# A gated recurrence block: decays scanned backward in place of their reciprocals, and the pooling's products made among the heads

## The chip, the cores and the metric

The kernel runs on one core of one Trainium2 chip. The metric is the device time of one execution in microseconds (us); three executions were timed before the change. One more execution was recorded by the hardware profiler: its page, and answers from its trace, are what this document quotes. PE is TensorE (matmuls), PEld its weight loads, DVE VectorE, ACT ScalarE, POOL GpSimd, and SP the queue that issues nearly all DMAs.

## The reference

One decoder layer on 1024 tokens of width 1024, all float32:

```python
proj = x @ w_in            # -> q, f, i, og, pool_v, gate_a, gate_b, each 1024 wide
# recurrence, 8 heads of 128, in chunks of 16 tokens:
qf = silu(q) * 128**-0.5;  f = lb + (1 - lb) * sigmoid(f);  k = 1 - f;  G = cumsum(log f) within a chunk
scores = tril((qf * exp(G)) @ (k * exp(-G)).T);   o_intra = scores @ v
state = exp(G_last) * state + (k * exp(G_last - G)).T @ v;   o_inter = (qf * exp(G)) @ state
o = rmsnorm_per_head(o_intra + o_inter) * g * sigmoid(og);   a = o @ w_a
# pooling, 4 groups of 256 channels, windows 2, 4, 8, 16:
pooled = causal_mean_w(pool_v) - pool_v;   b = (pooled @ w_pool[group]) * pool_scale
mix = (sigmoid(gate_a) * a + sigmoid(gate_b) * b) @ w_out
x = layer_norm(alpha * x + mix);   x = layer_norm(alpha * x + relu(x @ w_up)**2 @ w_down)
```

## The kernel before, in words

**Products.** Every float32 operand is split into a high and a low part (a cast on ACT, a subtraction on DVE), and each product takes three matmuls: high by high, high by low, low by high. The large products of `x` come in pairs by a Strassen scheme: `pair` (its matmuls in `prod`, L199 to L201) makes two output blocks for both halves of the tokens with seven products p1 to p7 of 12 matmuls of 512 columns. Each product needs its weights as a high and a low tile of 128x512. These tiles, made by `split` (L117 on ACT, L118 on DVE), come from a ring `w` of `NW` = 10 buffers; results wait in PSUM banks `pj` (four), and then in tiles `c`.

**Stages.** First the values `i` by rows (up to about 125 us). Then the heads: for each head `h`, `head_inputs(h)` makes q and f by one `pair`, and `hgrn(h, u, ...)` runs the recurrence for each half `u` of the tokens (a "unit"). In between stand the passes that `EXTRAS` lists: `output_gates` (the gate og of two heads), `pooled(g)` for g = 0 to 3 after heads 0 to 3, `gates(j)` (gate_a and gate_b of 128 channels) from head 4 on, `o_sums` (sums of heads' outputs), and at the end `pool_products(g)`. After the heads the mixer multiplies by w_a, gates and adds (`gated`, L983), and multiplies by w_out; layer norm, and the two products of the MLP follow.

**A unit.** `hgrn` makes the decays `fd` from f by a forward scan within chunks of 16 (two scans of 256 columns, L808), `k = 1 - f`, the reciprocal `r = 1/fd` (four instructions, L814), `q*fd`, `kc = k*r`, `kr = kc*T` with `T` the decay of a whole chunk, and several scaled copies of them for larger blocks of tokens. Transposes, scores (L884, L895), a masked copy (`copy_predicated`, L902), products with `v` (L872, L912, L915), the norm on ACT (L920 to L925) and a transpose back follow.

**The pooling.** `pooled(g)` makes pool_v of 256 channels by a `pair`; as its blocks come, `mean` adds shifted copies (one to four additions and a last operation for each quarter, L741 and L748, in tiles `pA` and `pC`) and each of four results `c` is stored to `po`. `pool_products(g)` loads them again at the end, loads the group's weights, splits both (the weights into rings `q`, `f`, `og`, `v` of the heads, the pooled tiles into the ring `w`), makes 24 matmuls (`mm3`, L104 to L106), multiplies by `pool_scale` and by the gate (`gb`, stored by `gates` and loaded again) in one DVE instruction (L726), and stores `pb`. For the last group the gate is not yet there: there ACT scales (L724), and `gates(7)` multiplies.

**Order.** The program is recorded in the order of the code, and a scheduler then orders each engine's instructions by priority (earlier code first) and hands out the buffers of each ring. Engines take their instructions in that order. The last unit has a raised priority.

Of the kernel before, what the change touches and what calls it, by code (L numbers as in the profile page):

```python
# [9 lines left out]
F32 = mybir.dt.float32  # L10
# [32 lines left out]
def tile_hybrid_block(  # L43
# [348 lines left out]
    def dram(name, width=HALF):  # L392
        return hd.tile([P, width], F32, tag=name, name=name)
# [181 lines left out]
    gad = [[dram(f"ga{j}_{u}") for u in range(2)] for j in range(8)]  # L575
    gbd = [[dram(f"gb{j}_{u}") for u in range(2)] for j in range(8)]
    pod = [[dram(f"po{j}_{u}") for u in range(2)] for j in range(8)]
    pbd = [[dram(f"pb{j}_{u}") for u in range(2)] for j in range(8)]
# [36 lines left out]
    with tc.tile_pool(name="tmp", bufs=1, side="right", reuse_waits="tile") as tmp:  # L615
        starts = hgp.tile([P, NB // 2, SUB], F32, name="starts")
        G.memset(starts, 0.0)
        G.memset(starts[:, :, 0:1], 1.0)
        att = [hgp.tile([P, CH, P], F32, name=f"att{i}") for i in range(1)]
        for t in att:  # L620
# [6 lines left out]

        RINGS = dict(q=3, f=3, og=2, v=2, tA=2, tC=2, st=2)

# [55 lines left out]
        def gates(j):  # L685
            spare = j == KT - 1
            rooms = [lambda tag=tag: tt(tag) for tag in ("q", "f", "og")] if spare else (c_soon, c_late, c_late)

            def take(dst, src=None, more=None):
                def put(t):  # L690
                    s = (tt("v") if spare else c_late()) if src else t
                    more_of = loaded(more, lambda: tt("v")) if more is not None else None
                    A.activation(s, t, AF.Sigmoid)
                    if more_of is not None:
                        V.tensor_mul(s, s, more_of)
                    nc.sync.dma_start(out=dst if more is None else more, in_=s)
                return put

            more = pbd[j] if spare else (None, None)
            run(pair(  # L700
                loaded_blocks(w_in, 5 * D + j * P, 6 * D + j * P), rooms,
                (take(gad[j][0]), take(gbd[j][0], True, more[0]), take(gad[j][1]), take(gbd[j][1], False, more[1])),
            ))

        def pool_products(g):

            tags = iter(("q", "f", "og", "v") * 3)

            def room(dtype=F32):
                return tt(next(tags), dtype)  # L710

            raw = raw_tile().rearrange("p k n c -> p (k n c)")[:, : 2 * 2 * P].rearrange("p (k c) -> p k c", c=2 * P)
            nc.sync.dma_start(out=raw, in_=w_pool[g].rearrange("(k p) c -> p k c", p=P))
            wh, wl = split(raw, lambda: room(F32R).rearrange("p (k c) -> p k c", c=2 * P))
            for u in range(2):
                pl = [split(loaded(pod[2 * g + i][u], room), row_tile) for i in range(2)]
                for i in range(2):
                    w = slice(i * P, (i + 1) * P)
                    j = 2 * g + i
                    t = room() if j == KT - 1 else loaded(gbd[j][u], room)  # L720
                    ps = ps_tile()
                    mm3(ps, [(wh[:, c, w], wl[:, c, w], *pl[c]) for c in range(2)])
                    if j == KT - 1:
                        A.activation(t, ps, AF.Copy, scale=pscale[:, j : j + 1])  # L724
                    else:
                        V.scalar_tensor_tensor(t, ps, pscale[:, j : j + 1], t, ALU.mult, ALU.mult)  # L726
                    nc.sync.dma_start(out=pbd[j][u], in_=t)

        def pooled(g):
# [3 lines left out]
            def mean(c, u):  # L733

                for lo in (QUARTER, 0):
# [12 lines left out]
                    V.scalar_tensor_tensor(pv[:, n:], cur[:, n:], 1.0 / win, pv[:, n:], ALU.mult, ALU.subtract)  # L748

            def put(c, i, u):  # L750
                nc.sync.dma_start(out=pod[j + i][u], in_=c[:, HALO:])

# [26 lines left out]
            def take_12(ps):  # L779
# [23 lines left out]
        def hgrn(h, u, ft, q, v, og, state):  # L803

            fd = tt("tA")
            for i in range(2):
                w = slice(i * QUARTER, (i + 1) * QUARTER)
                V.tensor_tensor_scan(fd[:, w], starts.rearrange("p b s -> p (b s)"), ft[:, w], 1.0, ALU.max, ALU.mult)  # L808
            k = ft
            A.activation(k, ft, AF.Identity, bias=cmask[:, P - 1 : P], scale=-1.0)  # L810
            r = tt("tC")
            for i in range(CH):
                w = slice(i * P, (i + 1) * P)
                V.reciprocal(r[:, w], fd[:, w])  # L814
            T = small("T", [P, NB])
# [26 lines left out]
            V.tensor_mul(blk(kr), blk(kc), bc(T, [P, NB, SUB]))  # L842
# [3 lines left out]
            V.tensor_mul(  # L846
                pairs_of(qc)[:, :, 0], pairs_of(q)[:, :, 0],
                bc(pairs_of(r)[:, :, 0, SUB - 1], [P, NB // 2, SUB]),
            )
# [89 lines left out]
        EXTRAS[7, 1] = (  # L939
            ("gates", 4), ("o_sums", 2), ("pool_products", 0), ("gates", 5), ("pool_products", 1), ("gates", 6), ("pool_products", 2), ("pool_products", 3), ("gates", 7),  # L940
        )
        nxt = head_inputs(0, (None, None, "p6", None, None))
        output_gates(0)
        for h in range(HEADS):
            fs, qs = nxt
            state = None
            for u in range(2):
                v, og = values(h, u), loaded(ogd[h][u], lambda: tt("og"))
                with tc.high_priority(PRIO_LAST) if (h, u) == (HEADS - 1, 1) else nullcontext():
                    state = hgrn(h, u, fs[u], qs[u], v, og, state)  # L950
                    if (h, u) == (HEADS - 1, 1):
                        tags = iter(("tD", "tE", "tF", "tC"))
                        o_sums(h - CH, lambda: tt(next(tags)))
                if h + 1 < HEADS and u:
                    nxt = head_inputs(h + 1)
                    if h % 2:
                        output_gates(h + 1)
                for what, j in EXTRAS.get((h, u), ()):
                    dict(gates=gates, pooled=pooled, pool_products=pool_products, o_sums=o_sums)[what](j)

# [438 lines left out]
```

## Time and profile before

| | us |
|---|---|
| median of three executions | 1463.76 |
| lowest, highest | 1461.53, 1465.18 |
| span of the profiled execution, first to last instruction | 1462.4 |
| PE busy | 1440.6 |
| DVE busy | 1140.0 |
| ACT busy | 756.9 |

The profiled execution's own time is known by its span alone. A row of the page's groups reads: line, engine, operation, output and inputs by the program's names, shapes, count, then after the bar busy time in us, mean of one instruction in ns, and after the second bar the engine's idle time before these instructions with what ended it. A row of waits reads: engine, tile and line that waited, for whom, then total us, times, longest. A row of the stretches reads: from and to, length, then busy time of each engine with its count of instructions, the clock granted to PE, the busy share of the DMA engines, and GB/s. A row of the timeline reads: start, duration, engine, line, operation, and how many in a row.

### The profile page before, as it was taken

The numbers are of one execution on the slowest core, as the hardware profiler recorded it, in microseconds if no ns is written. First come the engines' busy times: TensorE is split into PE (matmuls) and PEld (weight loads), VectorE is DVE, ScalarE is ACT, GpSimd is POOL, SyncE is SP. The second block draws the span as 40 slices with busy tenths as digits, with TensorE's granted clock in tenths as the row PEclk, the third lists the DMA queues.
The fourth block names the chain that finished last, engine by engine and source line by source line (L and its number), as shares of the span: only waits on it lengthen the run. The fifth ranks groups of instructions, "written<-read, shape, count | busy, mean of one in ns | idle before, by whom it ended". The sixth has DMA issues, their size and how long they took to land.

```text
span 1462.4 us, 20665 instructions
## 1 busy us (share of the span) xinstructions
PE 1440.6 (99%) x7377; PEld 1187.2 (81%) x7377; DVE 1140.0 (78%) x1838; ACT 756.9 (52%) x1383; POOL 63.5 (4%) x244
## 2 busy tenths in 40 slices
PE   9999999999999999999999999999999999999997
PEld 7888888888888888777888878888888888888886
DVE  5968989899998695767985598666666787777977
ACT  5445565665656566455442366555555443333535
POOL 0002000001000020000002100000000100000000
PEclk9999999999999999999999999999999999999999
DMA  7232233223333537987563135445464874445422
GB/s 252 75 120 87 88 100 103 94 87 109 95 109 108 168 122 248 345 285 238 186 226 135 69 98 195 133 150 172 144 232 156 284 267 146 160 135 170 128 72 115
DMA packets 160615, 226.82 MB, mean 155 GB/s; under 512 B 11232, under 2 KB 84480, under 8 KB 160512
## 3 DMA queue, kind: packets, MB, share of 16 engines
q1 hardware_dynamic: 158576, 218.93, 45.1%
q0 software_dynamic: 1152, 4.19, 0.8%
q10 hardware_dynamic: 784, 2.38, 0.5%
q8 instruction: 58, 0.95, 0.3%
q14 instruction: 45, 0.37, 0.1%
HBM read 154.16 MB, written 71.30 MB: 154 GB/s over the span
## 4 chain that ended last, share of the span: by engine, by line
PE 87%; DVE 5%; DMA 4%; ACT 2%; issue 1%; SPq 0%; DVEq 0%; ACTq 0%
PE ps_pj L199 14%; PE ps_pj L200 14%; PE ps_pj L201 14%; PE ps_pj L1282 4%; PE ps_pj L1281 4%; PE ps_pj L1280 4%; PE ps_pj L104 2%; PE ps_pj L105 2%; PE ps_pj L106 2%; PE ps_tr L1282 1%; PE ps_tr L1281 1%; PE ps_tr L1280 1%; PE ps_hg L199 1%; PE ps_sc L199 1%; PE ps_hg L200 1%
## 5 line engine op out<-in xcount | busy, mean ns | idle before, releaser
L199 PE MATMUL ps_pj<-act,w 128*128 128x512 f32 x1068 | 419.9, 395 | 6.4 <-ACT w L117 2.0
L200 PE MATMUL ps_pj<-act,w 128*128 128x512 f32 x1068 | 417.3, 391 | 0.5 <-DVE act L123 0.5
L201 PE MATMUL ps_pj<-act,w 128*128 128x512 f32 x1068 | 411.8, 392 | 0.1
L199 PEld LDWEIGHTS ps_pj<-act,w 128*128 128x128 f32 x1068 | 200.3, 188 | 52.4 <-ACT w L117 3.9
L201 PEld LDWEIGHTS ps_pj<-act,w 128*128 128x128 f32 x1068 | 200.4, 188 | 42.9 <-DVE w L118 1.4
L200 PEld LDWEIGHTS ps_pj<-act,w 128*128 128x128 f32 x1068 | 200.6, 188 | 41.0 <-DVE act L123 0.9
L117 ACT CAST w<-t 128x512 fp32r<-128x512 f32 x170 | 104.7, 619 | 115.5 <-PE ps_pj L200 52.1
L118 DVE TENSOR_TENSOR w<-raw,w 128x512 fp32r<-128x512 f32 x143 | 99.3, 700 | 62.3 <-ACT w L117 48.4
L117 ACT CAST w<-raw 128x512 fp32r<-128x512 f32 x143 | 88.3, 620 | 96.1 <-PE ps_pj L200 45.4
L118 DVE TENSOR_TENSOR w<-t,w 128x512 fp32r<-128x512 f32 x170 | 116.4, 688 | 26.2 <-ACT w L117 23.3
L1242 ACT CAST act<-act 128x1024 fp32r<-128x1024 f32 x66 | 67.0, 1051 | 108.9 <-issue 35.0
L1282 PE MATMUL ps_pj<-act,act 128*128 128x512 f32 x240 | 93.0, 389 | 0.0
L1281 PE MATMUL ps_pj<-act,act 128*128 128x512 f32 x240 | 93.0, 389 | 0.0
L1243 DVE TENSOR_TENSOR act<-act,act 128x1024 fp32r<-128x1024 f32 x66 | 79.4, 1221 | 17.3 <-ACT act L1242 17.3
L1280 PE MATMUL ps_pj<-act,act 128*128 128x512 f32 x240 | 92.4, 389 | 0.0
L272 DVE TENSOR_TENSOR c<-c,ps_pj 128x512 f32<-128x512 f32 x95 | 64.7, 682 | 28.9 <-PE ps_pj L201 23.7
L268 ACT COPY c<-ps_pj 128x512 f32<-128x512 f32 x96 | 55.3, 584 | 11.3 <-PE ps_pj L201 10.4
L814 DVE RECIPROCAL tC<-tA 128x128 f32<-128x128 f32 x64 | 54.6, 910 | 0.0
L1281 PEld LDWEIGHTS ps_pj<-act,act 128*128 128x128 f32 x240 | 45.0, 188 | 9.4
L1280 PEld LDWEIGHTS ps_pj<-act,act 128*128 128x128 f32 x240 | 45.0, 188 | 9.3
L1282 PEld LDWEIGHTS ps_pj<-act,act 128*128 128x128 f32 x240 | 45.0, 188 | 9.3
L238 DVE TENSOR_TENSOR t<-raw,raw 128x512 f32<-128x512 f32 x43 | 29.6, 689 | 18.0 <-DMA raw<-in_w_in_dram 14.2
(415 smaller groups left out, 2728.3 us busy)
## 6 DMA issues: line engine op xcount, KB each, us to landing
h<-c SPq DMA_DIRECT2D x106, 256.0 KB, 2.4
act<-h SPq DMA_DIRECT2D x78, 256.0 KB, 3.0
raw<-in_w_in_dram SPq DMA_DIRECT2D x64, 256.0 KB, 3.4
draw<-in_w_down_dram SPq DMA_DIRECT2D x16, 1024.0 KB, 8.3
raw<-in_w_up_dram SPq DMA_DIRECT2D x30, 512.0 KB, 4.2
raw<-in_w_in_dram SPq DMA_DIRECT2D x18, 512.0 KB, 3.9
hf<-h SPq DMA_DIRECT2D x34, 256.0 KB, 3.0
c<-o SPq DMA_DIRECT2D x24, 256.0 KB, 3.8
```

The source lines that it names most:

```text
L117: A.copy(hi, src)
L118: V.tensor_sub(lo, src, f(hi))
L199: PE.matmul(ps, wh[:, k], th, start=first and k == 0, stop=False, skip_group_check=True)
L200: PE.matmul(ps, wh[:, k], tl, start=False, stop=False, skip_group_check=True)
L201: PE.matmul(ps, wl[:, k], th, start=False, stop=k == CH - 1, skip_group_check=True)
L268: A.copy(t, ps)
L272: V.tensor_add(t, t, ps)
L1242: A.copy(hi, src)
L1243: V.tensor_sub(lo, src, f(hi))
L1280: PE.matmul(ps, hh[:, w], wh, start=fresh and n == 0, stop=False, skip_group_check=True)
L1281: PE.matmul(ps, hh[:, w], wl, start=False, stop=False, skip_group_check=True)
L1282: PE.matmul(ps, hl[:, w], wh, start=False, stop=n == M - 1, skip_group_check=True)
```

## The change

In `hgrn` the reciprocals of all decays go. The decay from a token to its chunk's end, `to_end`, is made by a scan that runs backward over f (two scans, of 255 and 256 columns); `kr = k*to_end` directly; only the 32 chunk decays are inverted (`rT`), and half of `kc` comes from `kr` times `rT`. `to_end` has one buffer `tC` (it was two) and is later overwritten by `ke`.

`pooled(g)` keeps its four results on the chip and calls `pool_products(g, po)` itself, so these products now stand among heads 0 to 3. Weights of the group are loaded into `tF` (one buffer, also that of `qc` in `hgrn`), and their parts go into the ring `w`, as those of the pooled tiles. ACT multiplies by `pool_scale` and the result is stored to `pb`. Each `gates(j)` first loads its two tiles of `pb` into `pA` and `pC` (each one buffer), multiplies them with the gate and stores `pb` again. `po` and `gb` are no longer stored.

```diff
-        RINGS = dict(q=3, f=3, og=2, v=2, tA=2, tC=2, st=2)
+        RINGS = dict(q=3, f=3, og=2, v=2, tA=2, st=2)
...
         def gates(j):
             spare = j == KT - 1
             rooms = [lambda tag=tag: tt(tag) for tag in ("q", "f", "og")] if spare else (c_soon, c_late, c_late)
+            more = [loaded(pbd[j][u], lambda tag=tag: tt(tag)) for u, tag in enumerate(("pA", "pC"))]
-            def take(dst, src=None, more=None):
+            def take(dst, src=None, more_of=None):
                 def put(t):
                     s = (tt("v") if spare else c_late()) if src else t
-                    more_of = loaded(more, lambda: tt("v")) if more is not None else None
                     A.activation(s, t, AF.Sigmoid)
                     if more_of is not None:
                         V.tensor_mul(s, s, more_of)
-                    nc.sync.dma_start(out=dst if more is None else more, in_=s)
+                    nc.sync.dma_start(out=dst, in_=s)
                 return put
...
-                (take(gad[j][0]), take(gbd[j][0], True, more[0]), take(gad[j][1]), take(gbd[j][1], False, more[1])),
+                (take(gad[j][0]), take(pbd[j][0], True, more[0]), take(gad[j][1]), take(pbd[j][1], False, more[1])),
...
-        def pool_products(g):
+        def pool_products(g, po):
-            raw = raw_tile().rearrange("p k n c -> p (k n c)")[:, : 2 * 2 * P].rearrange("p (k c) -> p k c", c=2 * P)
+            raw = tt("tF").rearrange("p (k c) -> p k c", c=2 * P)
             nc.sync.dma_start(out=raw, in_=w_pool[g].rearrange("(k p) c -> p k c", p=P))
-            wh, wl = split(raw, lambda: room(F32R).rearrange("p (k c) -> p k c", c=2 * P))
+            wh, wl = split(raw, lambda: row_tile().rearrange("p (k c) -> p k c", c=2 * P))
             for u in range(2):
-                pl = [split(loaded(pod[2 * g + i][u], room), row_tile) for i in range(2)]
+                pl = [split(po[i][u], row_tile) for i in range(2)]
                 for i in range(2):
                     w = slice(i * P, (i + 1) * P)
                     j = 2 * g + i
-                    t = room() if j == KT - 1 else loaded(gbd[j][u], room)
                     ps = ps_tile()
                     mm3(ps, [(wh[:, c, w], wl[:, c, w], *pl[c]) for c in range(2)])
-                    if j == KT - 1:
-                        A.activation(t, ps, AF.Copy, scale=pscale[:, j : j + 1])
-                    else:
-                        V.scalar_tensor_tensor(t, ps, pscale[:, j : j + 1], t, ALU.mult, ALU.mult)
+                    t = c_late()
+                    A.activation(t, ps, AF.Copy, scale=pscale[:, j : j + 1])
                     nc.sync.dma_start(out=pbd[j][u], in_=t)
...
             def put(c, i, u):
-                nc.sync.dma_start(out=pod[j + i][u], in_=c[:, HALO:])
+                po[i][u] = c[:, HALO:]
...
+            pool_products(g, po)
...
+            to_end = tt("tC")
+            G.memset(to_end[:, HALF - 1 :], 1.0)
+            V.tensor_tensor_scan(
+                to_end[:, HALF - 2 : QUARTER - 1 : -1], ft[:, HALF - 1 : QUARTER : -1], first_of[:, 1:],
+                1.0, ALU.mult, ALU.max,
+            )
+            V.tensor_tensor_scan(
+                to_end[:, QUARTER - 1 :: -1], ft[:, QUARTER : 0 : -1], first_of, 0.0, ALU.mult, ALU.max,
+            )
             k = ft
             A.activation(k, ft, AF.Identity, bias=cmask[:, P - 1 : P], scale=-1.0)
-            r = tt("tC")
-            for i in range(CH):
-                w = slice(i * P, (i + 1) * P)
-                V.reciprocal(r[:, w], fd[:, w])
+            rT = small("rT", [P, NB])
+            V.reciprocal(rT, blk(fd)[:, :, SUB - 1])
...
+            kr = tt("tE")
+            V.tensor_mul(kr, k, to_end)
             kc = tt("tD")
-            V.tensor_mul(kc, k, r)
-            kr = tt("tE")
-            V.tensor_mul(blk(kr), blk(kc), bc(T, [P, NB, SUB]))
             A.copy(pairs_of(kc)[:, :, 0], pairs_of(kr)[:, :, 0])
+            V.tensor_mul(pairs_of(kc)[:, :, 1], pairs_of(kr)[:, :, 1], bc(rT2[:, :, 1], [P, NB // 2, SUB]))
...
-            ke = tt("tC")
+            ke = to_end
...
         EXTRAS[7, 1] = (
-            ("gates", 4), ("o_sums", 2), ("pool_products", 0), ("gates", 5), ("pool_products", 1), ("gates", 6), ("pool_products", 2), ("pool_products", 3), ("gates", 7),
+            ("gates", 4), ("o_sums", 2), ("gates", 5), ("gates", 6), ("gates", 7),
         )
```

More of the change, by code (lines that the diff above doesn't have):

```diff
@@ L575, in tile_hybrid_block @@
     gad = [[dram(f"ga{j}_{u}") for u in range(2)] for j in range(8)]
-    gbd = [[dram(f"gb{j}_{u}") for u in range(2)] for j in range(8)]
-    pod = [[dram(f"po{j}_{u}") for u in range(2)] for j in range(8)]
     pbd = [[dram(f"pb{j}_{u}") for u in range(2)] for j in range(8)]
@@ L618, in tile_hybrid_block @@
         G.memset(starts[:, :, 0:1], 1.0)
+        first_of = starts.rearrange("p b s -> p (b s)")
         att = [hgp.tile([P, CH, P], F32, name=f"att{i}") for i in range(1)]
@@ L807, in hgrn @@
                 w = slice(i * QUARTER, (i + 1) * QUARTER)
-                V.tensor_tensor_scan(fd[:, w], starts.rearrange("p b s -> p (b s)"), ft[:, w], 1.0, ALU.max, ALU.mult)
+                V.tensor_tensor_scan(fd[:, w], first_of, ft[:, w], 1.0, ALU.max, ALU.mult)
+            to_end = tt("tC")
[7 more added lines that the diff above has]
+            )
             k = ft
             A.activation(k, ft, AF.Identity, bias=cmask[:, P - 1 : P], scale=-1.0)
-            r = tt("tC")
-            for i in range(CH):
-                w = slice(i * P, (i + 1) * P)
-                V.reciprocal(r[:, w], fd[:, w])
+            rT = small("rT", [P, NB])
+            V.reciprocal(rT, blk(fd)[:, :, SUB - 1])
+            rT2 = rT.rearrange("p (b e) -> p b e", e=2)
             T = small("T", [P, NB])
@@ L847, in hgrn @@
                 pairs_of(qc)[:, :, 0], pairs_of(q)[:, :, 0],
-                bc(pairs_of(r)[:, :, 0, SUB - 1], [P, NB // 2, SUB]),
+                bc(rT2[:, :, 0], [P, NB // 2, SUB]),
             )
@@ L958, in tile_hybrid_block @@
                 for what, j in EXTRAS.get((h, u), ()):
-                    dict(gates=gates, pooled=pooled, pool_products=pool_products, o_sums=o_sums)[what](j)
+                    dict(gates=gates, pooled=pooled, o_sums=o_sums)[what](j)
         hg_scope.close()
```

5 lines of the change are left out of this document (1 added, 4 removed).

## The prediction

> **What bounds the kernel now.** I read the page first, its busy line and its chain of waits.
>
> ```profile
> PE 1440.6 (99%) x7377; PEld 1187.2 (81%) x7377; DVE 1140.0 (78%) x1838; ACT 756.9 (52%) x1383; POOL 63.5 (4%) x244
> PE 87%; DVE 5%; DMA 4%; ACT 2%; issue 1%; SPq 0%; DVEq 0%; ACTq 0%
> ```
>
> PE is busy nearly throughout, and the chain that ended last runs over PE. But records of matmuls overlap, so 99% hides lost time. The second view, busy time by stretch, counts matmuls: the heads (125 to 585), the end of the mixer (585 to 700), two short stretches in it, and one of the up-projection for scale.
>
> ```profile
> core 0: us, PE busy (x) PEld busy (x) DVE busy (x) ACT busy (x) POOL busy (x), PEclk, DMA share, GB/s
> 125.00:585.00 460.00, 457.26 (x3008) 377.10 (x3007) 401.84 (x784) 279.04 (x626) 41.41 (x194) 1.00 0.37 117
> 585.00:700.00 115.00, 109.50 (x466) 87.56 (x465) 84.59 (x135) 57.31 (x104) 0.00 (x0) 0.99 0.87 293
> 683.00:686.30 3.30, 1.72 (x5) 1.01 (x6) 3.30 (x6) 3.30 (x7) 0.00 (x0) 1.00 0.98 344
> 686.30:689.80 3.50, 3.50 (x11) 2.71 (x10) 3.50 (x7) 1.26 (x3) 0.00 (x0) 0.51 1.00 334
> 1000.00:1050.00 50.00, 50.00 (x221) 41.17 (x221) 29.84 (x46) 26.41 (x46) 0.00 (x0) 1.00 0.48 157
> ```
>
> Where nothing is late, 221 matmuls of 512 columns take 50 us, 0.226 us each. At that rate the 466 of the end of the mixer (all of 512 columns) need 105.3 us; they took 115, so 9.7 us are lost there. In the heads DVE is busy for 401.84 of 460 us (87%): the second engine, close behind PE. Third, PE's waits, first in the heads, then at the end of the mixer:
>
> ```profile
> PE ps_pj L199 <- ACT w L117: 1.2, 1, 1.2
> PE ps_pj L199 <- ACT c L268: 1.1, 2, 0.7
> PE ps_pj L199 <- DVE c L272: 0.4, 1, 0.4
> ...
> PE ps_pj L199 <- ACT act L122: 1.6, 1, 1.6
> PE ps_pj L104 <- ACT w L117: 1.4, 1, 1.4
> PE ps_pj L199 <- ACT w L117: 0.8, 1, 0.8
> PE ps_pj L199 <- ACT f L724: 0.6, 1, 0.6
> ```
>
> In 460 us of heads PE waits 2.7 us. So a lighter DVE there can give 2.7 us at most; the end of the mixer can give 9.7.
>
> **Removed and added on DVE.** The prices:
>
> ```profile
> L814 DVE RECIPROCAL tC<-tA 128x128 f32<-128x128 f32 x64 | 54.6, 910 | 0.0
> L808 DVE TENSOR_TENSOR_SCAN tA<-starts,f 128x256 f32<-128x256 f32 x32 | 20.3, 676 | 2.7 <-ACT f L651 1.6 <-PE ps_hg L915 1.1
> L842 DVE TENSOR_TENSOR tE<-tD,T 128x512 f32<-128x512 f32 x16 | 11.0, 687 | 0.0
> L851 DVE TENSOR_TENSOR tE<-tE,T 128x256 f32<-128x256 f32 x16 | 6.8, 422 | 0.0
> L741 DVE TENSOR_TENSOR pA<-c 128x271 f32<-128x271 f32 x32 | 13.9, 435 | 0.1
> L880 DVE SCALAR_TENSOR_TENSOR st<-st,dec,ps_hg 128x128 f32<-128x128 f32 x48 | 16.3, 339 | 1.2 <-PE ps_hg L872 1.0
> L902 DVE COPY_PREDICATED att<-cmask,sc 128x512 f32<-128x512 uint32 x16 | 11.9, 743 | 1.7 <-PE ps_hg L912 1.6
> L726 DVE SCALAR_TENSOR_TENSOR q<-ps_pj,prm,q 128x512 f32<-128x512 f32 x8 | 6.0, 747 | 1.0 <-PE ps_pj L106 1.0
> 418.26 3.36 DVE L814 RECIPROCAL tC<-tA 128x128 f32<-128x128 f32 x4
> ```
>
> Four reciprocals of 910 ns in a row take 3.36 us, so a record overlaps the next by 0.09 us; I take 0.09 off every mean: 0.82 for a reciprocal, 0.59 for a scan, 0.60 for 512 columns, 0.33 for 256, 0.34 for one of the pooling's (435), 0.25 for 128 columns (L880), 0.65 for L902 and for the gating of a head's output (as L726). A unit (one head, half the tokens) loses four reciprocals (3.3) and the two 512-wide products for kc and kr (1.2), and gains two backward scans (1.2), one 512-wide product (0.6), one of 256 columns (0.33) and a reciprocal of 32 columns (by L814's rate 0.2): 2.2 us less, 35 us over 16 units. A scan with a negative step is nowhere in the trace; I take the forward scan's price, because it moves as many elements. At twice that, the unit still gains 1 us. By the 2.7 us above, the 35 us are worth 0 to 2.7; I take 1.5.
>
> The pool's products leave the end of the mixer. There they cost 96 matmuls (21.7 us of PE, which only move), and waits of their own: 1.4 (L104) and 0.6 (L724). Their DMAs go from there too: 16 pooled tiles and 14 gates no longer come in, the 4 weights and 16 stores of products move among the heads, and the DMA engines stand at 0.87 now. The gates' passes gain 14 products and 14 loads, ten of each in this stage: 6 us of DVE, which idles for 30 of the 115. So 2.0 us go for certain, 9.7 at most; I take 5.5.
>
> **What the moved products do among the heads.** In the order of the built program each pool_products holds ten tiles of the ring w: two of the weights and eight of the pooled tiles. The ring has ten (NW). On ACT the first cast for the next head's weights therefore stands behind the cast of the last pooled tile, which waits for DVE's mean of it:
>
> ```
> 413 L117 TensorCopy w_798<-c_752 [waits DVE]
> 414 L926 Activation tH_852<-ps_hg_850,ss_851
> 416 L117 TensorCopy w_856<-raw_854 [waits DMA]
> ```
>
> So four times, for g = 0 to 3, there is a hole: DVE makes no weight for a large product between the pooling's last (w_767 here) and the next head's first (w_857), while it does both units of a head and the pooling's means. In the kernel before, weights for large products stand at most 20 instructions apart in the heads; in the holes 63 to 83. Each hole, from the addition that frees the first pooled tile (L272) to the next head's first weight:
>
> - g=0: 19 of 512 columns, 16 of the pooling's, 4 scans, 8 of 256, 11 of 128, and 8 others: 26.7 us
> - g=1: 17, 24, 4, 6, 10 and 9: 28.0 us
> - g=2: 20, 32, 4, 8, 11 and 11: 33.8 us
> - g=3: 17, 40, 4, 6, 10 and 10: 33.6 us
>
> (at the prices above; of the others two to three are masked copies and a gating at 0.65, the rest reciprocals of 4 or 32 columns at 0.2 and edges at 0.1). PE in the same hole has five large products of 12 and the pool's 24 matmuls, 84 at 0.226 (19.0 us), and the small matmuls of two units:
>
> ```profile
> 205.40 1.06 PE L872 MATMUL ps_hg<-v,tH 128*128 128x128 f32 x8
> 208.70 0.46 PE L884 MATMUL sc<-tF,tD 128*32 128x32 f32 x32
> 209.35 0.68 PE L895 MATMUL sc<-q,k 128*64 128x64 f32 x8
> 238.62 0.49 PE L912 MATMUL ps_hg<-v,att 128*128 128x128 f32 x2
> 240.29 0.39 PE L915 MATMUL ps_hg<-st,tA 128*128 128x128 f32 x2
> ```
>
> For one unit: scores 1.33 (208.70 to 210.03), L912 and L915 1.83 (238.62 to 240.45), L872 0.9 net of overlap, transposes (eight of the same shape) 0.9: 5.0 us, for two 10.0. With 1 us of changes between shapes PE needs 30 us. DVE needs 3.3 and 2.0 us less in the first two holes, 3.8 and 3.6 more in the last two. That is a floor of 7.4 us of PE idle, in which DVE never waits. But it does (lines of the changed kernel): the second unit's L847 waits for the scores that read the one buffer tF, L903 for scores, L923 for squares and a table load on ACT. Behind each stand the pooling's means in DVE's order. And at the end come three steps of ACT.
>
> ```profile
> L117 ACT CAST w<-t 128x512 fp32r<-128x512 f32 x170 | 104.7, 619 | 115.5 <-PE ps_pj L200 52.1 <-DVE t L281 18.7 <-PE ps_hg L200 13.1
> L925 ACT ACTIVATE tH<-ps_hg,ss 128x128 f32<-128x128 f32 x64 | 18.3, 369 | 1.7 <-DVE ss L922 1.7
> L921 ACT ACT_TABLE_LOAD x16 | 20.5, 1283 | 0.3
> ```
>
> A cast (0.6), four norms (1.2) and the next head's cast (0.6) make up to 2.4 us. DVE idles 13% in the heads now; for all these waits together I take 10% of a hole, less than 13% because its backlog is long. That gives 29.4, 30.8, 37.2 and 37.0 us against 30: 0, 0.8, 7.2 and 7.0, together 15.0. The floor is 7.4; with 13% and all 2.4 us in each hole it is 2.6 + 4.0 + 10.6 + 10.4 = 27.6.
>
> PE's clock: after 683 to 686.3 with PE busy 1.72 of 3.30 us the granted clock was 0.51 for 3.5 us, and 11 matmuls took 3.5 us in place of 2.5. A hole's end, with sparse small matmuls, looks like that; 0 to 4 times 1.0 us, I take 2 (the two long holes). [...]
>
> **The sum.** 15.0 + 2 - 5.5 - 1.5 = 10 us more. The profiled span of 1462.4 becomes 1472.4. It lies among the runs (1461.53 to 1465.18), 1.4 under their median of 1463.76, and what lies around it is unchanged: 1474. Lowest: 7.4 - 9.7 - 2.7 = -5.0, 1459. Highest: 27.6 + 4 - 2.0 = 29.6, 1493.
>
> **Rivals.** First, faster: the holes close and the end of the mixer pays. PE's reserve of five large products lasts until DVE comes back; for it speaks that the first two holes have 2 to 3 us of slack on the floor. It decides where DVE gets through a long hole within 30 us, that is where scans and means run 10% under my prices, or where PE's small matmuls take longer than I count. Then -5.5 - 1.5 gives 1457, with all of 9.7 and 2.7 gone 1451. Against it: 83 instructions, and the chain after the last large product, which no other product of the program covers. Chance 0.20.
>
> Second, no change: the holes cost about what the end of the mixer gives, 1460 to 1468. That they cancel needs the floor of 7.4 with the 7.0 of gains I took: 1464. Chance 0.14. [...]
>
> Third, much slower: the ring also holds back the gates' loads, since SP issues in order and each gates pass loads into pA and pC, which the pass before must have read. If each of seven such loads kept SP by the 0.7 us that a product takes, 5 us more; with everything else at its highest, 1498. In the order these loads stand right behind the store that follows the reader, so it is unlikely: 0.05.
>
> **How the numbers follow.** A measurement of this kernel tells about 0.3% (4.4 us) from no change. Forecast and third rival give slower 0.66 (0.61 and 0.05), no change 0.14, faster 0.20. The likeliest is 1474, its own range by floor and ceiling of the holes 1466 to 1486; the range for eight in ten reaches into the first rival, 1458 to 1489.
>
> **What would show it.** In the changed kernel's profile: four stretches between 150 and 480 us in which PE's matmuls thin out while DVE is full, each ending with a wait of PE for L117 (w), longer for the third and fourth; PE's waits in the heads at 10 us or more in place of 2.7; a granted clock under 1.00 there. At the end of the mixer some 370 matmuls (466 less 96) and no L104 wait, the stage some 27 us shorter (21.7 moved, 5.5 gained). No L117 wait over 1 us in the heads would make the forecast wrong, and so would backward scans far from 676 ns.

## The result and the profile after

The changed kernel takes 1516.12 us (median of 4 runs, 1514.18 to 1517.2) against 1462.91 for the kernel before (4 runs, 1461.53 to 1465.18): a ratio of 1.0354, 95% interval 1.034 to 1.0367. That is 53 us slower, where 10 were forecast. The profiled execution took 1514.18 us, its span is 1512.3. First the busy line and the chain of waits on its page:

```profile
PE 1458.2 (96%) x7377; PEld 1200.1 (79%) x7377; DVE 1115.5 (74%) x1822; ACT 757.5 (50%) x1389; POOL 89.0 (6%) x260
...
PE 88%; DVE 4%; ACT 3%; DMA 2%; issue 1%; SPq 0%; POOL 0%; DVEq 0%; ACTq 0%
```

PE has the same 7377 instructions, DVE is 24.5 us lighter, and the span is 49.9 us longer. PE is still what the chain runs over; all that was added is time in which PE waits or has its matmuls further apart, at half clock above all (30.7 us of the stretch from 125 to 450). Next, busy time by stretch: most of the heads, and the 325 us behind them, which hold the last heads and the mixer's end.

```profile
core 0: us, PE busy (x) PEld busy (x) DVE busy (x) ACT busy (x) POOL busy (x), PEclk, DMA share, GB/s
125.00:450.00 325.00, 298.98 (x1870) 244.25 (x1870) 250.57 (x524) 173.32 (x400) 37.49 (x138) 0.95 0.27 87
...
450.00:775.00 325.00, 310.61 (x1715) 253.75 (x1714) 237.56 (x420) 176.27 (x356) 29.16 (x73) 0.98 0.53 170
```

Between 125 and 450 us PE issued 1870 matmuls, and the granted clock was 0.95. The same 325 us of the kernel before hold 2151 at a clock of 1.00:

```profile
125.00:450.00 325.00, 322.64 (x2151) 265.25 (x2150) 300.67 (x601) 194.21 (x437) 31.69 (x160) 1.00 0.31 96
```

PE's waits in that stretch of the changed kernel (engine, tile and line that waited, who ended it; total, times, longest):

```profile
PE ps_tr L929 <- ACT tH L926: 7.9, 3, 3.5
PE sc L885 <- DVE tD L844: 5.8, 2, 3.5
PE ps_pj L104 <- ACT w L117: 2.5, 3, 1.2
PE ps_pj L199 <- ACT w L117: 2.3, 1, 2.3
PE ps_hg L913 <- DVE att L903: 2.3, 2, 1.4
PE ps_hg L913 <- DVE st L881: 2.0, 1, 2.0
```

With three smaller groups that is 25.8 us, where the prediction's view of before had 2.7 in all the heads. Most of these rows (tH, tD, att, st) are steps inside a unit: PE stands at one step of a head's recurrence and has no large product to run beside it.

To put a size on all of it I took for every form of matmul its median distance from start to start, and called what exceeds it lost. Over the span the kernel before loses 47 us so, the changed kernel 97. Of the difference, 37.6 us lie in the first four heads (125 to 450 against 125 to 425 before: 56.7 and 19.1) and 11.8 in the 325 and 300 us behind them (29.9 and 18.1).

### The profile page after: what moved, and what is told of

Its sections match the earlier page's. It is cut to its first block, busy times and chain, and to the rows that moved or that the text cites. A ratio compares the mean times of both kernels' runs of the same rounds, so it can differ in the third digit from the quotient of the medians.

```text
span 1512.3 us, 20648 instructions
## 1 busy us (share of the span) xinstructions
PE 1458.2 (96%) x7377; PEld 1200.1 (79%) x7377; DVE 1115.5 (74%) x1822; ACT 757.5 (50%) x1389; POOL 89.0 (6%) x260
## 4 chain that ended last, share of the span: by engine, by line
PE 88%; DVE 4%; ACT 3%; DMA 2%; issue 1%; SPq 0%; POOL 0%; DVEq 0%; ACTq 0%
PE ps_pj L199 15%; PE ps_pj L200 15%; PE ps_pj L201 15%; PE ps_pj L1282 4%; PE ps_pj L1283 4%; PE ps_pj L1281 4%; PE ps_pj L104 3%; PE ps_pj L105 2%; PE ps_pj L106 2%; PE ps_tr L1282 1%; PE ps_tr L1283 1%; PE ps_tr L1281 1%; PE ps_sc L199 1%; PE ps_hg L913 1%; PE ps_hg L199 1%; PE ps_sc L201 1%
## 5 line engine op out<-in xcount | busy, mean ns | idle before, releaser
L117 ACT CAST w<-t 128x512 fp32r<-128x512 f32 x170 | 105.3, 622 | 123.3 <-PE ps_pj L200 72.1
L117 ACT CAST w<-raw 128x512 fp32r<-128x512 f32 x143 | 87.9, 620 | 101.7 <-PE ps_pj L200 57.0
L268 ACT COPY c<-ps_pj 128x512 f32<-128x512 f32 x96 | 55.4, 584 | 14.4 <-PE ps_pj L201 9.7
L1146 ACT ACTIVATE c<-c 128x512 f32<-128x512 f32 x46 | 29.1, 633 | 21.5 <-DVE c L272 21.5
```

The costliest lines, as they stand in the source:

```text
L117: A.copy(hi, src)
L268: A.copy(t, ps)
```

## Experiments

**Which half of the change.** The diff has two halves that can be made alone: the unit's arithmetic, and the pool's products among the heads. First the arithmetic in the kernel before, hgrn as a whole as it is changed. (Line numbers in the rows of a run are those of its own file; the tiles' names tell the step.)

```
-        RINGS = dict(q=3, f=3, og=2, v=2, tA=2, tC=2, st=2)
+        RINGS = dict(q=3, f=3, og=2, v=2, tA=2, st=2)
...
+            to_end = tt("tC")
...
-            ke = tt("tC")
+            ke = to_end
```

> The kernel before with only the unit's arithmetic changed: backward scans and the reciprocals of 32 block ends in place of the 512 reciprocals, one buffer tC. The pool's products stay at the end of the mixer. Theory A (the changed kernel loses its 53 us because the pool's products hold the ring w, and PE has nothing large to fill the units' chains with): the scans alone cost nothing, DVE has 35 us less work, PE's waits in the heads stay near 2.7 us, time 1459 to 1464 us. Rival B (the new order inside a unit is what PE waits for: a longer chain from f to the scores, one buffer tC): a loss of 1 to 3 us in each of 16 units here too, time 1479 us or more.

Measured 1472.42 us, ratio 1.0056 (1.0043 to 1.0068). Neither theory's figure: 8.7 us slower, not nothing, and far from 53. The other half is the changed kernel with hgrn as it was before:

```
-            to_end = tt("tC")
...
+            r = tt("tC")
+            for i in range(CH):
+                w = slice(i * P, (i + 1) * P)
+                V.reciprocal(r[:, w], fd[:, w])
...
-            ke = to_end
+            ke = tt("tC")
```

> The changed kernel with the unit's old arithmetic (512 reciprocals, one buffer tC because two do not fit), the pool's products among the heads. Theory A: it loses what the changed kernel loses and more, because DVE has 2.2 us more per unit inside the holes (4.4 us a hole, some 18 us in four): 1520 to 1540 us. Rival B (the scans cost): it comes out well under the changed kernel's 1516 us, toward 1470.

Measured 1516.69 us, ratio 1.0359 (1.0345 to 1.0373). The pool's half of the change costs the whole 53 us without the scans; rival B falls. This run keeps the single buffer of tC and the tiles pA and pC of the gates passes, so the figure isn't that of the products alone. DVE's longer units (267.24 us of DVE in 125 to 450, against 250.57) made it no worse, against what theory A said.

Why do the scans cost 8.7 us when DVE has less to do? The changed arithmetic keeps ke in the buffer that the backward scan wrote, and tC is one buffer. With a second one:

```
-        RINGS = dict(q=3, f=3, og=2, v=2, tA=2, st=2)
+        RINGS = dict(q=3, f=3, og=2, v=2, tA=2, tC=2, st=2)
...
-            ke = to_end
+            ke = tt("tC")
```

> The kernel before with the scans, as in the first run, but with the two buffers of tC that it had, ke in the second. Theory S1 (the 8.7 us that the scans alone cost come from the single buffer: a unit's backward scan waits for the transposes of ke of the unit before): back to 1460 to 1466 us. Theory S2 (they come from a shifted order: the mixer's end starts with other transfers in flight, 4.5 us of the 8 lie there): 1469 to 1474 us, as with one buffer.

Measured 1466.95 us (12 runs, 1463.72 to 1469.79), ratio 1.0022 (1.0011 to 1.0033), just above theory S1's range: 5.5 of the 8.7 us are the buffer. The view of the tile tC says what idled before its instructions; the same row of the run with one buffer, of this run, and of the changed kernel:

```profile
  PE ps_tr L876: 81.3, 10
```

```profile
  PE ps_tr L876: 3.5, 2
```

```profile
  PE ps_tr L868: 100.6, 10
```

With one buffer GpSimd's memset, which opens a unit's backward scan, waits ten times for the transposes of ke of the unit before, 81.3 us in all (100.6 in the changed kernel). With two that is 3.5. How this wait reaches PE isn't shown. The 3.1 us left over I can't place; the profiled execution can't show them, since it was the fastest of the twelve, level with the kernel before.

**What makes the holes.** The next two runs cut the question in the middle. One keeps all the work and takes the wait for the means away:

```
-                pl = [split(po[i][u], row_tile) for i in range(2)]
+                pl = [split(f(xp["a11"][2 * i + u][:, 0]), row_tile) for i in range(2)]
```

> The changed kernel, the pool's products made at the same place, of the same number, with the same ten buffers, casts and subtractions; but they take a tile that has lain on chip since the start in place of the pooled tile just made (left out: the pooled tiles reach no product). Only the wait for DVE's means is gone. Theory A2 (the next head's weights wait behind the last pooled tile, which waits for DVE's last mean): the longest stretches in DVE's order without a weight for a large product fall from 64 to 85 instructions to 37 to 45, the lost time in the first four heads falls by half or more, 1482 to 1494 us. Rival D (it is the amount of work there, whenever the inputs are ready): 1508 to 1516 us.

Measured 1481.73 us, ratio 1.0125 (1.0106 to 1.0144), 0.3 us under theory A2's range: 34.4 us of the 53 are gone, with the same products at the same place. The stretch of the heads and its waits:

```profile
125.00:450.00 325.00, 319.48 (x2060) 260.98 (x2059) 273.03 (x575) 199.13 (x439) 46.57 (x162) 0.99 0.30 95
```

```profile
PE ps_pj L199 <- ACT w L117: 2.4, 3, 1.7
PE sc L885 <- DVE tD L844: 1.8, 1, 1.8
PE ps_pj L199 <- ACT c L268: 1.2, 1, 1.2
```

2060 matmuls in the 325 us in place of 1870, the clock back at 0.99, and 5.4 us of waits in place of 25.8. By the count of distances the first four heads lose 26.8 us in place of 56.7. The pooled tiles also give up their c tiles sooner here, but no lack of c tiles went with it: PE's wait for them (L268) is 1.2 us, and 1.4 in the changed kernel. The other run takes the products away:

```
         def pool_products(g, po):
...
             for u in range(2):
...
                 for i in range(2):
...
+                    nc.sync.dma_start(out=pbd[2 * g + i][u], in_=po[i][u])
```

> The changed kernel without the pool's 96 products and their 20 tiles' parts (left out: the pooled tiles go to the gates as they are). 21.7 us of PE's work are gone with them. If all that the first four heads lose comes from the products' place: lost time there as with the scans alone, 30 us less than in the changed kernel, 1516 - 21.7 - 30 = 1464, or 1458 to 1468 us. If the scans with one buffer, or the pooled tiles staying on chip, lose there without the products too: 1475 to 1494 us.

(The load of the weights, all parts, the 96 matmuls and ACT's scaling go.) Measured 1458.58 us, ratio 0.996 (0.9944 to 0.9975), inside the first range. With the 21.7 us of the products' own PE time added that is 1480.3, within 1.5 us of the run with ready inputs. So the work of the products costs about what its PE time says, 21.7 us; what costs 34 more is that their tiles are still being made by DVE. Rival D falls.

Next, how that wait reaches the other products. Four buffers of the ring set free:

```
-                pl = [split(po[i][u], row_tile) for i in range(2)]
+                pl = [row_tile() for i in range(2)]
+                for i in range(2):
+                    A.copy(pl[i], po[i][u])
...
-                    mm3(ps, [(wh[:, c, w], wl[:, c, w], *pl[c]) for c in range(2)])
+                    for c in range(2):
+                        PE.matmul(ps, wh[:, c, w], pl[c], start=c == 0, stop=False)
+                        PE.matmul(ps, wl[:, c, w], pl[c], start=False, stop=c == 1)
```

> The changed kernel without the low parts of the pooled tiles (left out: 32 of the pool's 96 products and 16 subtractions on DVE), so that a group holds six buffers of the ring w and four stay free. Theory A1 (the ring is full: with buffers free the next head's weights are made): two pairs of weights, 24 products or 5.4 us, go into each hole, and the 32 products less give up to 7.2 us: 1516 - 22 - 7 = 1487, or 1484 to 1496 us. Theory A2 (not how many buffers but in which order the ring gives them out: a head's weight gets its buffer after the last pooled tile has its own, and that waits for DVE's last mean): the next head's first weight comes as late as before, the holes stay, and only what the 32 products cost at the holes' ends is saved: 1508 to 1516 us.

Measured 1507.21 us, ratio 1.0299 (1.028 to 1.0318), within 1 us of theory A2's range, and the same waits inside the units:

```profile
PE ps_tr L933 <- ACT tH L930: 8.3, 3, 3.5
PE sc L889 <- DVE tD L848: 6.1, 2, 3.7
```

Theory A1 falls: it isn't that the ring is full. The 8.9 us are little more than the 7.2 of the products left out. So two rings, one for the pooled tiles alone (in the first four heads all other weights then have six buffers in place of ten; elsewhere the ten are handed out in turn):

```
-        return wq.tile([P, CH, P], F32R, tag="w", name=nm("w"), bufs=NW)
+        return wq.tile([P, CH, P], F32R, tag=tag, name=nm("w"), bufs=dict(w=6, p=4)[tag])
...
-                pl = [split(po[i][u], row_tile) for i in range(2)]
+                pl = [split(po[i][u], lambda: row_tile("p")) for i in range(2)]
```

> The changed kernel with the same ten buffers in two rings, six for the heads' weights and w_pool's, four for the pooled tiles' parts alone; all the arithmetic is there. Theory A2: the head's weights no longer stand behind the pooled tiles, two pairs of them (24 products) can be made in the hole; in DVE's order the longest stretches without a weight for a large product fall from 64 to 85 instructions to 32 to 55, and the lost time of the first four heads from 57 us to 30 to 40: 1493 to 1503 us. Rival (DVE's sum of work sets the holes): no change, 1512 to 1518. Rival (six buffers are too few for the heads): slower than 1518.

Measured 1531.97 us, ratio 1.047 (1.045 to 1.049): 16 us slower than the changed kernel, where only the rival with too few buffers put it. The waits are the units' own again, and longer:

```profile
PE sc L891 <- DVE tD L850: 7.3, 3, 5.6
PE ps_hg L919 <- DVE st L887: 7.3, 2, 5.1
PE ps_hg L919 <- DVE att L909: 5.8, 2, 3.3
```

The next head's first two pairs of weights were indeed made early (in the third hole at 331.5 and 334.7 us; six buffers less w_pool's two allow no more), but PE ran their products at once, ahead of the hole, and then stood in it with nothing. Here weights that came early were no help, because they were few. What a ring of their own would do with ten buffers left to the heads, this run doesn't show.

**Deferring the products.** The products one head later, from tiles stored and loaded again:

```
-                po[i][u] = c[:, HALO:]
+                nc.sync.dma_start(out=pod[j + i][u], in_=c[:, HALO:])
...
-        EXTRAS = {(h, 1): (("pooled", h),) for h in range(4)}
+        EXTRAS = {(h, 1): (("pool_products", h - 1), ("pooled", h)) if h else (("pooled", h),) for h in range(4)}
+        EXTRAS[4, 1] = ("pool_products", 3), ("gates", 0)
```

> The changed kernel, but the pooled tiles are stored to DRAM as before and loaded again, and each group's products come one head later, behind the next head's weights, not ahead of them; DVE's and PE's work is the same, SP has 32 more issues. Theory A (order on the ring w): the four holes close, PE's lost time in the first four heads falls from 57 us to 19 to 25, time 1478 to 1490, the rest being the end of the mixer. Rival D (the holes come from DVE's sum of work in that stretch, wherever the products stand): little changes, 1508 to 1520. Rival E (the products lack at the end, and DVE is the bound): between, 1490 to 1508.

Measured 1507.97 us, ratio 1.0305 (1.0291 to 1.0319): 8 us less, not 30, on the border between rivals D and E. The waits changed hands:

```profile
PE ps_pj L104 <- ACT w L117: 7.8, 6, 2.4
PE ps_pj L105 <- DVE w L118: 3.5, 2, 2.0
```

Now the pool's products themselves wait for their loaded tiles, whose loads stand on SP's queue behind stores of gates that are not made yet (at 373.15 us two such stores held SP for 2.88 us, and the tiles' loads followed). With the two rings, earlier loads and the last gates pass on v:

```
+        def pool_load(g):
+            raw = c_late().rearrange("p (k c) -> p k c", c=2 * P)
+            nc.sync.dma_start(out=raw, in_=w_pool[g].rearrange("(k p) c -> p k c", p=P))
+            ahead[g] = raw, [loaded(pod[2 * g + i][0], lambda: tt("pA" if i == 0 else "pC")) for i in range(2)]
...
+        for h in range(4):
+            EXTRAS[h + 1, 0] = (("pool_load", h),)
...
                     nxt = head_inputs(h + 1)
+                    if h - 1 in ahead:
+                        pool_products(h - 1)
```

> The changed kernel with the pooled tiles' parts in a ring of their own (as in the run before), each group's products one head later from tiles stored to DRAM and loaded ahead of use (into pA, pC and a c tile), behind the next head's weights, and the last gates pass loading into v. No arithmetic is left out. In DVE's order no stretch of the first four heads is longer than 27 instructions without a weight for a large product. Theory A2: the holes close, 57 us of lost time there become 19 to 25, and 9.5 us go at the end: 1516 - 35 - 9 = 1472, or 1466 to 1478 us. Rival D (DVE's work and the units' latencies set the holes, whatever the order): 1490 us or more.

Measured 1492.58 us, ratio 1.0198 (1.018 to 1.0216): at the low end of rival D's range, 15 us above theory A2's. Less the 9.5 us of the last gates pass (below) the deferral gives 14. In the first four heads the lost time falls by 18 us, from 56.7 to 38.2; behind 775 us it grows by 6, from 3.7 to 9.7. Rival D's mechanism isn't what is left, though: the units' waits are nearly gone, and most of the rest is the pool's products (L105) waiting for the casts of their loaded tiles:

```profile
PE ps_pj L105 <- ACT w L118: 9.1, 4, 6.5
PE ps_pj L200 <- ACT c L274: 1.4, 2, 0.9
PE ps_hg L925 <- DVE st L893: 1.1, 1, 1.1
```

Two things held the cast behind the longest of these waits (423.79 to 430.24 us): the tile's load, issued at 426.55 when DVE's last mean had released pA, and a step of the unit ahead of it on ACT, which waited 3.69 us for DVE's scan, until 428.96. Two attempts on those waits failed. All tiles loaded ahead, the second half into c tiles:

```
-            ahead[g] = raw, [loaded(pod[2 * g + i][0], lambda: tt("pA" if i == 0 else "pC")) for i in range(2)]
+            ahead[g] = raw, [
+                [loaded(pod[2 * g + i][u], c_late if u else lambda: tt("pA" if i == 0 else "pC")) for i in range(2)]
+                for u in range(2)
+            ]
```

> As the deferred kernel with rings of its own and the last gates pass on v (1492.6 us), but all four pooled tiles of a group are loaded ahead of use, the second half into c tiles. No arithmetic is left out. Theory (what is left in the first four heads, 38 us lost against 19 in the kernel before, is mostly the 9.5 us in which the pool's products wait for their loaded tiles, and the clock behind it): the waits for the second half go, 4 to 9 us less, 1484 to 1489. Rival (the wait is for the store of the tiles, which stands behind DVE's means on SP's queue, so loads issued earlier come no earlier): 1490 to 1494.

Measured 1511.15 us, ratio 1.0317 (1.0298 to 1.0336), above both figures. The wait for the fourth group's tiles grew, and the c tiles now lack elsewhere:

```profile
PE ps_pj L105 <- ACT w L118: 8.5, 1, 8.5
PE ps_hg L927 <- DVE st L895: 5.3, 1, 5.3
PE ps_pj L200 <- ACT c L274: 5.1, 5, 2.6
```

And with the fourth group one unit later and o_sums(2) one unit earlier:

```
-        for h in range(4):
+        for h in range(3):
             EXTRAS[h + 1, 0] = (("pool_load", h),)
-        EXTRAS[4, 1] = (("gates", 0),)
+        EXTRAS[4, 1] = ("gates", 0), ("pool_load", 3)
+        EXTRAS[5, 0] = (("pool_products", 3),)
...
-        EXTRAS[7, 0] = (("gates", 3),)
+        EXTRAS[7, 0] = ("gates", 3), ("o_sums", 2)
```

> As the run with all loads ahead, and two moves: the fourth group's products one unit later (behind the first gates pass), and the sums o_sums(2) one unit earlier, out of the last stretch of gates passes. No arithmetic is left out. Theory: the 6.5 us wait at 423 us and the 3.4 us wait for c tiles that the sums' stores hold at 633 us both go, with some of the half clock behind them: 10 to 14 us under the deferred kernel's 1492.6, 1478 to 1483. Rival (each only moves to another place): 1484 to 1494.

Measured 1500.37 us, ratio 1.0246 (1.0228 to 1.0265), above both figures, 11 us under the run before it and 8 over the one that it meant to better. No order that I tried has the pooled tiles ready early without taking a buffer or a place on a queue that something else needs.

**The last gates pass.** One edit in the changed kernel:

```
-            more = [loaded(pbd[j][u], lambda tag=tag: tt(tag)) for u, tag in enumerate(("pA", "pC"))]
+            more = [None if spare else loaded(pbd[j][u], lambda tag=tag: tt(tag)) for u, tag in enumerate(("pA", "pC"))]
...
+                    more_of_ = loaded(dst, lambda: tt("v")) if late else more_of
```

> The changed kernel with one edit: the last gates pass loads its two product tiles into v, as the kernel before did, at the moment of use, in place of pA and pC, whose memory the mixer's first weight tile takes over. Theory C (the mixer's first load of w_a waits for the last multiplication with pA; 6.3 us of PE idle at 706 us and 6.8 us at half clock at 722): the load goes out early, the 6.3 us wait goes, time 6 to 10 us less, 1506 to 1510. Rival (that load is late anyway, behind the stores and loads ahead of it on SP's queue): another wait of the same length stands in its place, 1514 to 1517.

Measured 1506.66 us, ratio 1.0295 (1.0281 to 1.0309): 9.5 us less, as theory C has it. In the changed kernel PE's longest waits behind 585 us, then SP's queue and ACT's cast at that place:

```profile
PE ps_pj L199 <- ACT w L117: 6.1, 1, 6.1
PE ps_pj L199 <- ACT c L268: 3.2, 2, 2.9
```

```profile
708.09 0.32 SPq L695 DMA_DIRECT2D pb<-v  x1
708.50 1.00 SPq L214 DMA_DIRECT2D raw<-in_w_a_dram  x2
```

```profile
712.14 1.14 ACT L117 CAST w<-raw 128x512 fp32r<-128x512 f32 x2 [4.80 <-DMA raw<-in_w_a_dram]
```

The mixer's first weights are loaded at 708.50, right behind the store of the last product that used pA and pC: they lie in the memory of the pool hgp, which the mixer's pool takes over. ACT waits 4.8 us for the load, PE 6.1 us for ACT. With v in their place those 6.1 us are gone, and these are left (at the first, 2.9 us long in the changed kernel, ACT's copy itself waited 4.6 us there for a store of `o_sums` to free its c tile):

```profile
PE ps_pj L199 <- ACT c L268: 3.0, 1, 3.0
PE ps_hg L199 <- ACT room L268: 2.5, 1, 2.5
```

Against waits of that kind I moved o_sums(2), in the kernel before with the scans and two buffers of tC, and it gave nothing:

```
-        EXTRAS[7, 0] = (("gates", 3),)
+        EXTRAS[7, 0] = ("gates", 3), ("o_sums", 2)
```

> The kernel before with the scans and two buffers of tC (1466.95 us), and o_sums(2) one unit earlier, so that its four loads and four stores leave the mixer's end, which loses 10 us to waits on transfers. No arithmetic is left out. If those waits come from these transfers: 2 to 5 us less, 1462 to 1465, level with the kernel before or just under. If they come from the mixer's own loads: unchanged, 1466 to 1468.

Measured 1470.45 us, ratio 1.0038 (1.0025 to 1.0052), above both figures and 3.5 us over the run without the move; the two intervals overlap, so that it is slower isn't shown, only that nothing was won.

**The account.** The wait for the means 34.4, pA and pC 9.5, the scans 8.7: 52.6 us of the 53. The first two are one edit each in the changed kernel. The third was measured in the kernel before. The run without the scans came out level with the changed kernel, but it keeps the single buffer and gives DVE more to do, so whether the 8.7 add there isn't shown; that the three meet the total may be partly chance. Which mechanism hands the wait on (the ring's order or the order on ACT and DVE, where the next head's first cast stands right behind the last pooled one) isn't separated: the run with two rings changed both. No version with all the arithmetic beat the kernel before.

## Why the prediction was wrong

**Right: the place, the length and DVE's work of the holes, and what opens them.** That the next head's weights stand behind tiles that wait for DVE's means is borne out by the run with ready inputs, which gives 34.4 us back. PE's waits rose past 10 us and the clock fell below 1.00, two of the signs named (25.8 us, and 0.95 from 125 to 450 us). From the pooling's last weight to the next head's first one on DVE, the four holes:

```profile
167.76:196.68 28.92, 23.87 (x214) 18.85 (x213) 26.14 (x65) 13.23 (x37) 2.58 (x15) 0.94 0.21 64
252.29:283.75 31.46, 28.17 (x238) 23.07 (x237) 27.86 (x69) 14.33 (x38) 4.05 (x16) 0.95 0.22 67
314.02:353.84 39.82, 31.19 (x240) 25.10 (x239) 33.26 (x83) 16.51 (x51) 4.36 (x19) 0.87 0.17 54
398.86:438.77 39.91, 33.18 (x250) 26.62 (x249) 34.29 (x87) 16.92 (x51) 2.97 (x15) 0.87 0.23 73
```

DVE is busy 26.14, 27.86, 33.26 and 34.29 us; the sums were 26.7, 28.0, 33.8 and 33.6. The holes are 28.92, 31.46, 39.82 and 39.91 us long; forecast 29.4, 30.8, 37.2 and 37.0. Together they are 5.7 us longer than that.

**Wrong: what PE has to do in them.** "With 1 us of changes between shapes PE needs 30 us" is the step that failed. Counted in the trace, the holes hold 54, 74, 69 and 80 matmuls of 512 columns in place of 84 (of the 60 of large products 42 to 56, because PE ran the others as soon as their weights existed, ahead of the hole; of the pool's 24 in the first two holes 12 and 18), and the small ones take 6.6 to 7.9 us for two units, not 10. At the median distances that is 93 us of work, not 120, in 140 us. So some 47 us are lost in the holes where 15 + 2 were forecast, with 4 more for changes between shapes (the author's estimate; no run shows this term by itself), and even the ceiling of 27.6 was too low. (Not all 47 are new: the kernel before loses 19.1 us in its first four heads by the same count.) The floor compared DVE's sum with PE's, as if whatever PE has could be spread over the hole. In the trace it wasn't: PE had run 4 to 18 of the 60 large products before the hole began, and in it stood at the units' steps, for 3.46 us at tH (until 340.27 us) and 3.45 at tD (until 190.85) the longest.

**Wrong: the sign that was to show it.** "Each ending with a wait of PE for L117 w": no hole ends with a head's large product waiting so. The one such wait, 2.3 us, lies between the first and the second hole:

```profile
236.08 0.75 PE L199 MATMUL ps_pj<-act,w 128*128 128x512 f32 x1 [2.32 <-ACT w L117]
```

The pool's own products (L104) do wait for L117 w in the last two holes, 2.5 us in three waits. The rest is spread over the units' steps, since PE meets those first.

**Wrong: the clock, 2 us (0 to 4).** Idle time accounts for 23.6 of the 37.6 us that the first four heads lose more than before; the other 14.0 are matmuls at a larger distance than the median, most of them at half clock, which held for 30.7 of the 325 us (granted clock 0.95).

**Wrong: the heads' other waits, -1.5.** A lighter DVE gave nothing, and the single buffer of tC, which the change's diff shows in RINGS and in ke, was not priced. The price of the scans held: the backward ones took 676 and 666 ns, the forward scan 676 before. The reciprocal of 32 columns took 0.34 us, 0.25 less the overlap, not 0.2, and with the scans alone DVE's busy time fell by 29 us (1140.0 to 1111.0), not 35.

```profile
L804 DVE TENSOR_TENSOR_SCAN tC<-f,starts 128x255 f32<-128x255 f32 x16 | 10.8, 676 | 0.0
L808 DVE TENSOR_TENSOR_SCAN tC<-f,starts 128x256 f32<-128x256 f32 x16 | 10.7, 666 | 0.0
L814 DVE RECIPROCAL rT<-tA 128x32 f32<-128x32 f32 x16 | 5.5, 341 | 0.1
```

**Wrong: the end of the mixer, -5.5.** The stretch that holds it lost 11.8 more. "2.0 us go for certain" priced what leaves the stage and not what takes its place: pA and pC in memory that the mixer needs next. The third rival looked at those two buffers, but at their loads on SP in the gates passes, not at who gets their memory. Without that the stretch is still some 2.3 us worse than before (11.8 less 9.5), with waits for transfers. What the stage holds was miscounted too: in the kernel before only nine of the 16 pooled tiles are loaded behind 585 us, and of the passes that gain products only gates(5) and gates(6) lie wholly there, with four products and not ten.

**Of the rivals** the faster one needed the holes to close, and none of the four did. The second needed the end of the mixer to give what the holes cost, and the stretch that holds it lost 11.8 us itself. Nothing came of a lighter DVE either: the run with the scans and two buffers is 3 us slower, not faster. The third was right that the change is much slower, and its 1498 was still 18 us short; the loads on SP that it named cost PE little, since PE waited for 0.8 us in all from 450 to 650 us, where most gates passes stand.

## What to carry to other kernels

The products that PE has beside the units' chains of short dependent steps filled its waits here where they were ready all through the chain (5.4 us of waits in 325 with ready inputs, 25.8 without): count what is ready when, not how much there is. Before moving work to an idle-looking place, ask when its inputs are made and what is queued behind it on every engine and ring; here the same 96 products cost their own 21.7 us with ready inputs, and 34 more with inputs that DVE was still making. When a buffer moves from one pool to another, or loses its second copy, price who takes that memory next (9.5 and 5.5 us here).

## What the runs showed of the hardware

From 125 to 450 us of the changed kernel the granted clock was 0.50 in six pieces: four of 3.41 us, one of 6.83 and one of 10.24. In the last 3.41 us of each piece PE was busy for 3.38 us or more, and behind it the clock was 1.00. In the fourth hole, the 3.40 us ahead of a piece, the whole piece, and its three parts of 3.41 us:

```profile
420.50:423.90 3.40, 1.27 (x57) 1.08 (x56) 2.75 (x8) 3.08 (x12) 0.10 (x1) 1.00 0.26 77
423.90:434.15 10.25, 7.57 (x31) 6.78 (x32) 8.72 (x23) 2.68 (x10) 0.10 (x1) 0.50 0.15 53
423.89:427.30 3.41, 2.77 (x11) 2.37 (x12) 2.68 (x6) 1.27 (x5) 0.10 (x1) 0.50 0.00 0
427.30:430.72 3.42, 1.37 (x6) 1.08 (x6) 2.70 (x11) 0.67 (x2) 0.00 (x0) 0.50 0.43 152
430.72:434.13 3.41, 3.41 (x17) 3.31 (x16) 3.34 (x8) 0.73 (x3) 0.00 (x0) 0.50 0.02 7
```

PE was busy 1.27 of 3.40 us with 57 matmuls, and the granted clock was 0.50 for the 10.25 us that followed. Behind the part with PE busy for 2.77 us the clock stayed at 0.50, behind the one with 3.41 it was 1.00. In the other three holes PE was busy for 0.82, 1.21, 1.18 and 1.13 of the 3.41 us ahead of half clock (from 188.37, 273.71, 328.32 and 338.56 us). What decides it, these rows don't show: behind 3.42 us with PE busy for 1.67 (from 335.14) the clock was 1.00, and in the kernel before it was 0.51 behind 3.30 us with 1.72. Behind the heads PE was idle for 6.11 us, up to 712.81 us, and the clock was 0.50 from 710.61 to 717.44 us.
